# The first expert product of a two-layer decoder in a fixed order: copies and activations reordered, gates four chunks later, top-k interleaved, rows and weight chunks loaded ahead into the activations' area

## The chip, the cores and the metric

The kernel runs on one core of one Trainium2 chip. The metric is device microseconds (us) of one execution, the median of several runs. In the text TensorE is PE, VectorE is DVE, ScalarE is ACT, GpSimd is POOL and SyncE is SP; SP, ACT and POOL also issue DMAs, each from a queue of its own, in order.

## What is computed

256 tokens of width 1024 go through two layers. Each layer has a mixing half (attention, convolution, spatial gating) and a PEER half: a product-key retrieval picks 16 of 16384 single-neuron experts for each of 8 heads of a token. The change lies in the PEER half, of which this is the reference, cut:

```python
q = (t @ w_pq).reshape(T, PEER_HEADS, 2, PEER_HALF)
s = jnp.einsum('thpk,hpnk->thpn', q, sub_keys)
top_s, top_i = lax.top_k(s, PEER_TOPK)                 # two times 16 of 128 keys
cand_s = top_s[:, :, 0, :, None] + top_s[:, :, 1, None, :]
best_s, best_pos = lax.top_k(cand_s.reshape(...), PEER_TOPK)
gate = jax.nn.softmax(best_s, axis=-1)
u = expert_down[experts]                               # rows of 1024
act = gelu(einsum('td,thkd->thk', t, u))
out = einsum('thk,thkd->td', gate * act, expert_up[experts])
```

Before each half the residual is normalised and scaled by vectors that come from six products of the conditioning vector with `w_ada` (48 columns of 1024 rows in each layer).

## The kernel before

The fp32 weights are streamed once, in chunks of 128x1024 values (512 KB each), through a ring of seven buffers (`raw`). `Src.seq` lists the chunks in the order of their use: `w_ada` columns ("ada"), input, output and query projections, then 128 chunks of `down` and 128 of `up` in each layer, with the `ada` columns that are due later spread among them. Half of the `down` and `up` chunks are issued on ACT's queue, the rest on SP's.

The PEER half of a layer works in three steps.

1. Query projection and top-k. Scores of both token blocks (128 tokens each, `b` = 1 and 0) go to DVE, which finds the top 16 keys (`top_keys`), sums the candidates, finds their top 16 (`top_cand`), turns positions into indices (`ranks`, `match`, `times`, `total`) and forms the softmax (`gate`). These steps lie in one list, `fill`, of which `run_fill` releases a budget after each chunk. `to_picks` then transposes the indices and gates of a block on PE and copies them out on ACT and DVE.
2. First product. For each of 128 `down` chunks PE multiplies the chunk with T tokens (`DENSE`: 168 in the first layer, 160 in the second), two chunks to a PSUM bank (`ch`, two buffers). ACT applies the gelu and writes `acts`, 128 x T values in the `arena`, the large SBUF tile in which all regions are cut. Meanwhile the gates are spread over the experts: for a group of four tokens DVE makes one-hots (`make_onehots`, L1021), ACT scales them (L1028 to L1032, and L1034 on DVE), PE multiplies them into a PSUM bank `g` (`gate_mm`, L1044), and `gate_use` multiplies the gelus already there (DVE, L1052) or lays the gate down for those to come (ACT, L1055). `act_use` (L1072) multiplies a later gelu (L1064, into `gt`) into gates that lie there.
3. The other 88 or 96 tokens (`TS`) are not in the dense product. For each of them POOL gathers 128 expert rows of 1024 values (`fetch`, L988, an indirect DMA of 512 KB) and DVE multiplies the rows with the token (`dot`, L998). This needs the picks of block 1 in another layout (`pairs`), which they reach through DRAM (`pair_in`), and the tokens repeated over the partitions, through DRAM too (`dot_in`). Second product (`combine`): PE multiplies `up` chunks with `acts` (L1083), DVE adds the gathered `up` rows (L1013), and `folds` (L1089) joins both.

What sets the order: up to the second product the tile framework's scheduler arranges the instructions of each engine by its own estimate, and only the second product and the passages between the halves are under `manual_schedule`, in the order of the code. The numbers that the code fixes are: dots from chunk `begin` + 6 to 120, `begin` = 21; gates from `start` = 28 to chunk 124; `FILL` and `FILL_DOWN`, the budgets of `run_fill`. Both layers have the same `begin` and `start`.

Of the kernel before, what the change touches and what calls it, by code (L numbers as in the profile page):

```python
# [44 lines left out]
PICKS_LAG = 3  # L45
D_FIRST = 6
D_LAST = 120
# [3 lines left out]
FILL = 1.25  # L51
FILL_DOWN = 2.1
EARLY = (112, 116, 96, 100, 64, 68)
ADA_TAIL = 0
# [15 lines left out]
def hybrid_trunk(ctx: ExitStack, tc: tile.TileContext, x_in, c_in, vec_in, w_ada, w_in, w_out, w_pq,  # L70
# [41 lines left out]
    dot_in = [dram.tile([S - t, D], F32, name=f"dot_in{n}") for n, t in enumerate(DENSE)]  # L112
    pair_in = [dram.tile([S - t, 2, P], F32, name=f"pair_in{n}") for n, t in enumerate(DENSE)]
# [63 lines left out]
    class Src:  # L177
# [4 lines left out]
        later = []  # L182

    def dma_ahead(upto):
        while Src.loaded < min(upto, len(Src.seq)):
            kind, src, raw = Src.seq[Src.loaded]
            if kind != "early":
                raw = stream.tile([P, D], F32, name="raw", tag="raw", bufs=RAW)
# [7 lines left out]
    fill = deque()  # L196

    def run_fill(budget):
        Src.credit = min(budget, Src.credit + budget)
        while fill and Src.credit > 0:  # L200
            cost, fn = fill.popleft()
            fn()
            Src.credit -= cost
# [14 lines left out]

    def cast_step(late=None):
# [4 lines left out]
        while Src.later and Src.later[0][0] <= k + RAW - QUEUE_LAG:  # L224
            nc.scalar.dma_start(*Src.later.pop(0)[1:])
# [3 lines left out]
        if kind == "ada":  # L229
# [24 lines left out]
        dma_ahead(k + RAW)  # L254
        return True

# [28 lines left out]
    for layer in range(DEPTH):  # L285
# [3 lines left out]
        if layer == 0:  # L289
# [7 lines left out]
            body = first[:2] + body[:n] + first[2:] + mix(body[n:] + tail[:ADA_TAIL], ada(0, [2, 3, 4])) + tail[ADA_TAIL:]  # L297
# [5 lines left out]
        if layer + 1 < DEPTH:  # L303
            dn = mix(dn, ada(0, [5]) + ada(1, [0, 1]), 4, 112)
            un = mix(un, ada(1, [2, 3, 4]), 4, 120)
        else:
            dn = mix(dn, ada(1, [5]), 40, 112)
        seq += dn + un
    Src.seq = seq
    dma_ahead(RAW)  # L310
# [168 lines left out]
    def tables(layer, after=None):  # L479
# [3 lines left out]
        nc.gpsimd.dma_start(R_BIAS, rel_bias)  # L483
        nc.gpsimd.dma_start(R_SW, sgu_w[layer])
        nc.gpsimd.dma_start(R_SB, sgu_b[layer])
# [14 lines left out]
    def mixing(layer, qg, update=None, late=None):  # L500
# [245 lines left out]
        if layer == 0:  # L746
# [3 lines left out]
            qg = tables(0, R_HF[:, 4, 0:1])  # L750
# [39 lines left out]
    def retrieval(layer, update, late):  # L790
        known.clear()
        T = DENSE[layer]
        def top_keys(b, hp):
            s = R_S[:, b, hp, :]
            v = R_TS[:, b, hp * 16:(hp + 1) * 16]
            ix = R_TI[:, b, hp * 16:(hp + 1) * 16].bitcast(U32)
            scr = R_SCR[:, hp % 2, :P]
            nc.vector.max(out=v[:, :8], in_=s)
            nc.vector.max_index(out=ix[:, :8], in_max=v[:, :8], in_values=s)
            nc.vector.match_replace(out=scr, in_to_replace=v[:, :8], in_values=s, imm_value=NEG_FILL)  # L800
            nc.vector.max(out=v[:, 8:], in_=scr)
            nc.vector.max_index(out=ix[:, 8:], in_max=v[:, 8:], in_values=scr)
# [11 lines left out]

        def cand(b):
# [9 lines left out]
        def top_cand(h):  # L825
            s = R_CAND[:, h, :]
            v = best[:, h * 16:(h + 1) * 16]
            ix = pos[:, h * 16:(h + 1) * 16].bitcast(U32)
            scr = R_SCR[:, h % 2, :80]
            nc.vector.max(out=v[:, :8], in_=s)  # L830
            nc.vector.max_index(out=ix[:, :8], in_max=v[:, :8], in_values=s)
            nc.vector.match_replace(out=scr, in_to_replace=v[:, :8], in_values=s, imm_value=NEG_FILL)
            nc.vector.max(out=v[:, 8:], in_=scr)
            nc.vector.max_index(out=ix[:, 8:], in_max=v[:, 8:], in_values=scr)
# [21 lines left out]
        def times(b, j):  # L856
            nc.vector.tensor_tensor(R_OH, R_OH, R_TE[:, b, :, j], op=OP.mult)
# [14 lines left out]

        def to_picks(b):
# [4 lines left out]
            if b == 1:  # L878
# [54 lines left out]
        def rest():  # L933
# [4 lines left out]
            for b in (1, 0):  # L938
                fill.append((0.7, lambda b=b: cand(b)))
                for h in range(8):  # L940
                    fill.append((0.8, lambda h=h: top_cand(h)))
# [352 lines left out]
```

## Time and profile before

| what | value |
|---|---|
| three runs | 1674.01, 1683.61, 1679.82 us; median 1679.82 |
| the profiled execution | 1675.43 us, its span 1673.7 us |
| PE, DVE, ACT, POOL busy | 93%, 61%, 26%, 29% of the span |
| DMA | 571.24 MB, mean 341 GB/s |
| first product, layer 0 and 1 | 189.1 to 558.0 us; 1032.5 to 1386.4 us |
| second product, layer 0 and 1 | 558.0 to 879.4 us; 1386.2 to 1669.4 us |

Busy shares are over the whole span. An engine with a low share can still be the one that is waited for, since engines work through their queues in order. Each `f32` matmul shows as two instructions in the trace, so a chunk is 16 of them.

### The profile page before, as it was taken

Reading aid. Unit: us, or ns where it says so; the run is one execution under the profiler, and the core shown is the slowest. Engines: PE = TensorE matmul, PEld = TensorE weight load, DVE = VectorE, ACT = ScalarE, POOL = GpSimd, SP = SyncE. Lnnn points to the kernel's source line nnn. Section 1 sums busy time; section 2 is a strip of 40 time slices with the busy share of each in tenths; the row PEclk is TensorE's granted clock in tenths of the full one; section 3 lists DMA queues with packets and bytes.
Section 4 is the critical chain, followed back from the end, with each engine's and each line's share of the span. In section 5 each row is a group of like instructions: output and inputs, shape, how many; then the busy total and the mean of one; then the engine's idle time right before and its main releaser. Section 6 shows DMA issues by size and latency. Waiting matters only on the chain.

```text
span 1673.7 us, 28977 instructions
## 1 busy us (share of the span) xinstructions
PE 1558.0 (93%) x11240; PEld 1520.5 (91%) x11240; DVE 1017.7 (61%) x2347; ACT 438.7 (26%) x1203; POOL 490.1 (29%) x441
## 2 busy tenths in 40 slices
PE   7999997988989999898999999969988899999998
PEld 6879987888989999898999899968988899999998
DVE  6757976767874154445436679767778743444443
ACT  2346223534343000000015763134344320000000
POOL 1000214434430243433300002054454404444440
PEclk9999998999999999999999999979999999999999
DMA  9975589999998999999975454889999989999997
GB/s 387 328 258 178 163 270 353 407 411 405 406 418 273 337 418 419 396 419 408 414 282 164 135 174 148 248 314 419 416 408 419 415 289 375 419 419 419 418 419 284
DMA packets 158461, 571.24 MB, mean 341 GB/s; under 512 B 20102, under 2 KB 20502, under 8 KB 157171
## 3 DMA queue, kind: packets, MB, share of 16 engines
q1 hardware_dynamic: 63072, 229.14, 37.0%
q0 software_dynamic: 58032, 205.16, 30.8%
q10 hardware_dynamic: 37219, 135.08, 21.2%
q8 instruction: 88, 1.44, 0.3%
q14 instruction: 50, 0.41, 0.1%
HBM read 565.20 MB, written 4.09 MB: 340 GB/s over the span
## 4 chain that ended last, share of the span: by engine, by line
PE 39%; DMA 32%; issue 13%; DVE 7%; POOL 6%; ACT 2%; SPq 0%; POOLq 0%; ACTq 0%; DVEq 0%
PE ch L316 13%; DMA arena<-in_up,arena 12%; PE acc L1083 12%; DMA arena<-in_down_rows,arena 5%; POOL arena L988 4%; DMA raw<-in_w_ada 4%; DMA raw<-in_up 3%; DMA spots<-in_up,arena 3%; DMA raw<-in_down 2%; PE ch L318 2%; PE ch L319 1%; PE ch L320 1%; POOL spots L988 1%; DMA pair_in<-chosen 1%; DMA spots<-in_down_rows,arena 1%
## 5 line engine op out<-in xcount | busy, mean ns | idle before, releaser
L316 PE MATMUL ch<-arena,raw 128*128 128x160 f32 (+2 forms) x4256 | 642.9, 312 | 21.1 <-ACT arena L1061 16.5
L316 PEld LDWEIGHTS ch<-arena,raw 128*128 128x128 f32 x4256 | 619.3, 195 | 28.7 <-ACT arena L1061 18.2
L1083 PE MATMUL acc<-arena,raw 128*128 128x168 f32 (+1 forms) x4096 | 578.9, 305 | 15.0 <-DMA raw<-in_up 14.8
L1083 PEld LDWEIGHTS acc<-arena,raw 128*128 128x128 f32 x4096 | 576.1, 192 | 17.1 <-DMA raw<-in_up 16.9
L988 POOL DMA_INDIRECT arena<-in_up,arena x154 | 193.5, 1257 | 351.3 <-DVE spots L1013 108.2
L1013 DVE SCALAR_TENSOR_TENSOR spots<-arena,spots 128x1024 f32<-128x1024 f32 x150 | 192.6, 1284 | 129.5 <-DMA arena<-in_up,arena 127.5
L206 DVE SCALAR_TENSOR_TENSOR raw<-raw,arena 128x1024 f32<-128x1024 f32 x96 | 116.6, 1219 | 177.3 <-DMA raw<-in_w_ada 135.5
L988 POOL DMA_INDIRECT arena<-in_down_rows,arena x134 | 152.1, 1135 | 194.4 <-DVE arena L998 170.3
L998 DVE SCALAR_TENSOR_TENSOR arena<-arena,spots 128x1024 f32<-128x1024 f32 x134 | 163.2, 1224 | 52.9 <-DMA arena<-in_down_rows,arena 52.5
L1044 PE MATMUL g<-arena 128*128 128x128 f16 x656 | 54.0, 226 | 58.2 <-ACT arena L1055 47.1
L1061 ACT ACTIVATE arena<-ch 128x336 f32<-128x336 f32 (+35 forms) x122 | 40.7, 336 | 250.4 <-PE ch L316 190.6
L1044 PEld LDWEIGHTS <-arena 128*128 128x128 f16 x656 | 45.8, 99 | 65.5 <-issue 51.2
L318 PE MATMUL ch<-hh,hi 128*128 128x256 f32 x288 | 82.6, 289 | 2.0 <-DVE arena L436 1.9
L1028 ACT ACTIVATE arena<-arena,parts 128x128 f16<-128x128 f16 x164 | 64.5, 393 | 75.9 <-DVE arena L1021 75.9
L347 ACT ACT_TABLE_LOAD x6 | 7.7, 1283 | 292.0 <-DMA raw<-in_up 291.9
L319 PE MATMUL ch<-hh,lo 128*128 128x256 f32 x288 | 81.8, 284 | 0.0
L320 PE MATMUL ch<-hh,hi 128*128 128x256 f32 x288 | 81.7, 284 | 0.0
L988 POOL DMA_INDIRECT spots<-in_down_rows,arena x50 | 59.9, 1197 | 73.4 <-DVE spots L998 59.8
L998 DVE SCALAR_TENSOR_TENSOR spots<-spots 128x1024 f32<-128x1024 f32 x50 | 61.2, 1224 | 20.3 <-DMA spots<-in_down_rows,arena 20.2
L1021 DVE TENSOR_TENSOR arena<-iota,picks 128x1024 f16<-128x1024 f16 x82 | 56.5, 691 | 23.6 <-PE g L1044 21.8
L239 DVE TENSOR_TENSOR lo<-raw,hi 128x1024 fp32r<-128x1024 f32 x42 | 51.4, 1230 | 27.9 <-ACT hi L246 27.8
L1052 DVE SCALAR_TENSOR_TENSOR arena<-arena,g 128x112 f32<-128x112 f32 (+31 forms) x82 | 37.9, 463 | 47.6 <-ACT arena L1061 40.1
(234 smaller groups left out, 1614.1 us busy)
## 6 DMA issues: line engine op xcount, KB each, us to landing
raw<-in_down SPq DMA_DIRECT2D x128, 512.0 KB, 7.1
raw<-in_down ACTq DMA_DIRECT2D x128, 512.0 KB, 7.3
raw<-in_up SPq DMA_DIRECT2D x128, 512.0 KB, 8.0
raw<-in_up ACTq DMA_DIRECT2D x128, 512.0 KB, 8.2
raw<-in_w_ada SPq DMA_DIRECT2D x96, 512.0 KB, 7.9
raw<-in_w_pq SPq DMA_DIRECT2D x32, 512.0 KB, 3.6
raw<-in_w_in SPq DMA_DIRECT2D x26, 512.0 KB, 4.7
raw<-in_w_out SPq DMA_DIRECT2D x16, 512.0 KB, 4.6
```

Source lines behind the costliest of these rows:

```text
L206: nc.vector.scalar_tensor_tensor(raw, raw, 1.0, cact, op0=OP.mult, op1=OP.mult, accum_out=mods[layer][:, col:col + 1])
L316: nc.tensor.matmul(dst, hi[:, cols], k[0], start=start, stop=stop, **kw)
L318: nc.tensor.matmul(dst, hi[:, cols], k[0], start=start, stop=False, **kw)
L319: nc.tensor.matmul(dst, lo[:, cols], k[0], start=False, stop=False, **kw)
L320: nc.tensor.matmul(dst, hi[:, cols], k[1], start=False, stop=stop, **kw)
L988: nc.gpsimd.indirect_dma_start(out=held[n], out_offset=None, in_=rows if n >= TS else down_rows[:, :], in_offset=bass.IndirectOffsetOnAxis ...
L998: nc.vector.scalar_tensor_tensor(row, row, 1.0, R_DX[which(k)[0]], op0=OP.mult, op1=OP.mult, accum_out=R_DOTS[:, k:k + 1])
L1013: nc.vector.scalar_tensor_tensor(R_SUM[s], row, w, R_SUM[s], op0=OP.mult, op1=OP.add)
L1021: nc.vector.tensor_tensor(both, iota2[:, None, :, :].to_broadcast([P, 4, P, 2]), vals[:, :, None, :].to_broadcast([P, 4, P, 2]), op=OP.is_ ...
L1028: nc.scalar.activation(og[0][:, 0, i, :], oh[:, 0, i, :], AF.Copy, scale=parts[:, 0, t + i:t + i + 1])
L1044: nc.tensor.matmul(dst, og[j][:, i // 2, i % 2, :], on[:, i // 2, :, i % 2], start=j == 0, stop=j == 1)
L1083: nc.tensor.matmul(acc[d // 2][:, (d % 2) * S:(d % 2) * S + T], u[:, d * P:(d + 1) * P], acts[:, i, :], start=i == 0 and d % 2 == 0, stop= ...
```

## The change

The first product, too, stands under `manual_schedule`: its instructions run in the order of the code. The loop over the 128 chunks is written anew, and this goes with it:

- ACT: the gelu of a pair of chunks stands ahead of the scaling copies, which come a chunk after their one-hots (`make_onehots` is split into `compare` and `factors`). `act_use` follows a pair later, with two temporary buffers. In `gate_use` ACT's part stands ahead of DVE's. The last scaling moves from DVE to ACT (eight ACT copies in a group instead of six, and no DVE one).
- Gates start at `start` + 4, one group to a pair of chunks. `start` is 33 and 35, `begin` 11 and 12 (layer 0 and 1).
- Top-k: two key sets or four candidate sets are worked on side by side, step by step, and block 1's whole list goes ahead of block 0's.
- The DRAM detours `dot_in` and `pair_in` are replaced by copies from SBUF to SBUF on POOL's queue, one for each stretch of partitions: 2 and 2 for the first set of tokens, then 8 and 8, 16 and 16 in layer 0 (4 and 4 in layer 1).
- Rows: seven regions of the later `acts` area hold rows until the gates start, and a few regions more hold them afterwards. Dots run at 0.2 to a chunk until `start`, then 0.8 or 0.92. 83 of 88 and 94 of 96 are done in the first product, and the rest at the head of the second.
- Chunks: ten `down` chunks (numbers 4 to 13) have places of their own in the `acts` area.
- `ada`: eight columns of layer 0 move from its first product to its output projection. Layer 1's columns ("aside") use the `hi`/`lo` buffers rather than the ring: 22 in the first product of layer 0, 18 in its second, 8 in layer 1's first.

```diff
-PICKS_LAG = 3
-D_FIRST = 6
-D_LAST = 120
+PICKS_LAG = 2
+WHERE_LAG = 4
+SETS_LAG = (0, 6, 11)
+SETS_KNOWN = 17
+D_FIRST = 8
+DOT_SLOW = 0.2
+DOT_RATE = (0.8, 0.92)
+AHEAD_AT = (8, 12, 16, 36, 40, 44, 48, 52, 56, 60)
+PASSING = (36, 40, 44, 48, 52, 56, 60)
-FILL = 1.25
-FILL_DOWN = 2.1
+FILL = 1.5
+FILL_DOWN = (2.2, 2.1)
...
+            body += mix(tail[:6], ada(0, [5])) + tail[6:]
...
+        for n, at in enumerate(AHEAD_AT):
+            dn[AHEAD_FIRST + n] = ("early", dn[AHEAD_FIRST + n][1], region(at * S, D))
...
+        def spread_picks(s):
+            off, n = SETS[s]
+            for h in range(P // n):
+                nc.gpsimd.dma_start(pairs[h * n:(h + 1) * n, :, off:off + n],
+                                    chosen[T - P + off:T - P + off + n, :, h * n:(h + 1) * n])
...
+        manual.enter_context(tc.manual_schedule())
...
             chunk_mm(ps[:, j * S:(j + 1) * S], next_chunk(), T, R_HX)
-            if pend is not None:
-                act_use(*pend)
-                pend = None
             while waiting:
                 g, gp = waiting.pop(0)
                 gate_use(g, gp, 2 * pair)
                 gdone = g + 1
+            if j == 1:
+                tdone = 4 * gdone
+                pend.append((pair, gelu(pair, ps, tdone), tdone))
+                if len(pend) > 1:
+                    act_use(*pend.popleft())
+            while compared:
+                factors(compared.pop(0))
+            if make and made < NG:
+                compare(made)
+                compared.append(made)
+                made += 1
...
+                if i == begin + WHERE_LAG:
+                    where(0)
+                    known_to[0] = SETS[0][1]
+                    fetch()
...
+                if i >= begin + D_FIRST:
+                    due += DOT_SLOW if start is None else DOT_RATE[layer]
+                while dotted < min(TS, int(due), len(held)):
+                    dot(dotted)
+                    dotted += 1
...
-        manual.enter_context(tc.manual_schedule())
         late = []
-        update, qg = combine(layer, late)
+        update, qg = combine(layer, late, dotted)
```

Three places show how the order on an engine moves. The first is DVE in the middle of layer 0's first product, about two groups of gates before the change: the row dots are L998, the one-hots L1021, the gates' use L1052, the later gelus' use L1072, the scaling L1034.

```order
L998 SCALAR_TENSOR_TENSOR spots,arena<-spots 128x1024
L1021 TENSOR_TENSOR arena<-iota_85,picks 128x1024
L1052 SCALAR_TENSOR_TENSOR arena<-arena,g 128x62x4
L1072 TENSOR_TENSOR arena<-arena,gt 128x2x60
L1034 TENSOR_TENSOR arena<-arena,parts 128x256
L998 SCALAR_TENSOR_TENSOR arena<-arena,spots 128x1024 x3
L1052 SCALAR_TENSOR_TENSOR arena<-arena,g 128x64x4
L1021 TENSOR_TENSOR arena<-iota_85,picks 128x1024
L1072 TENSOR_TENSOR arena<-arena,gt 128x2x64
```

The same place on DVE after the change; L1048 is the dot, L218 an `ada` column, L1107 the gates' use, L1125 the later gelus' use and L1071 the one-hots.

```order
L1048 SCALAR_TENSOR_TENSOR spots,arena<-spots 128x1024
L218 SCALAR_TENSOR_TENSOR aside,mod_108<-aside,arena 128x1024
L1107 SCALAR_TENSOR_TENSOR arena<-arena,g 128x60x4
L1125 TENSOR_TENSOR arena<-arena 128x2x44
L1071 TENSOR_TENSOR arena<-iota_85,picks 128x1024
L1048 SCALAR_TENSOR_TENSOR arena<-arena,spots 128x1024 x2
L1107 SCALAR_TENSOR_TENSOR arena<-arena,g 128x62x4
L1125 TENSOR_TENSOR arena<-arena 128x2x48
```

Each pair now has the same order, gates, gelus, one-hots, dots, with one or two dots between two uses of gates where up to three stood; the scaling is gone from DVE, and the dots come last in their pair.

The second place is PE at the first gates of layer 0, before the change: the transposes of block 1's and block 0's picks (L876), `down` chunks (L316, here eight rows of `x` to a chunk), and the first gate products (L1044).

```order
L316 MATMUL ch<-arena,raw 128x168 x120
L876 MATMUL g<-ident,arena 128x128 x3
L316 MATMUL ch<-arena,raw 128x168 x64
L876 MATMUL g<-ident,arena 128x128 x3
L316 MATMUL ch<-arena,raw 128x168 x16
L1044 LDWEIGHTS arena
```

The same place on PE after the change (L918 the transposes, L345 the chunks, L1097 the gate products); chunks that lie in the arena alone are those loaded ahead.

```order
L345 MATMUL ch<-arena,raw 128x168 x8
L345 MATMUL ch<-arena 128x168 x80
L918 MATMUL g<-ident,arena 128x128 x3
L345 MATMUL ch<-arena,raw 128x168 x152
L918 MATMUL g<-ident,arena 128x128 x3
L345 MATMUL ch<-arena,raw 128x168 x48
L1097 LDWEIGHTS arena
```

Between the last picks and the first gates stood two chunks, and six stand there now; block 1's picks come nineteen chunks ahead of block 0's instead of eight.

The third place is SP's queue from the output projection of layer 0 to its first product, before the change.

```order
L192 DMA raw<-in_w_ada 128x1024 x3
L192 DMA raw<-in_w_out 128x1024 x8
L192 DMA raw<-in_w_pq 128x1024 x16
L192 DMA raw<-in_down 128x1024 x4
L192 DMA raw<-in_w_ada 128x1024
```

A piece of the same stretch after the change, in which the chunks loaded ahead are those that go to the arena.

```order
L204 DMA raw<-in_w_ada 128x1024 x2
L204 DMA raw<-in_w_out 128x1024 x2
L204 DMA raw<-in_w_pq 128x1024 x9
L204 DMA arena<-in_down 128x1024 x2
L204 DMA raw<-in_w_pq 128x1024 x2
L204 DMA arena<-in_down 128x1024 x2
```

The ten chunks now stand among the loads of the input, output and query projections (three, two and five of them), with projection weights behind them in the same queue.

More of the change, by code (lines that the diff above doesn't have):

```diff
@@ L962, in experts, with release @@
         R_DROW = spots[:, 3, :]
-        free = deque([spots[:, n, :] for n in range(len(SETS), 4)] + [region(108 * S, D)])
+        beyond = [region(at * S, D) for at in (80, 84) if at * S >= P * T]
+        passing = [region(at * S, D) for at in PASSING]
+        free = deque([spots[:, n, :] for n in range(len(SETS), 3)] + [region(108 * S, D)] + beyond + passing)
         held = {}
+        known_to = [0]
+        retired = []
+        def release(row):
+            if not any(row is r for r in retired):
+                free.append(row)
         def dot_rows():
@@ L1062, in gelu @@
             if tdone:
[L1063 removed]
+                tmp = region(120 * S + pair % 2 * 2 * T, 2, T)
                 nc.scalar.activation(tmp[:, :, :tdone], v[:, :, :tdone], AF.Gelu)
@@ L1152, in experts @@
                 start = i + 1
-                make_onehots(0)
-                make_onehots(1)
+                for g in range(2):
+                    compare(g)
+                    compared.append(g)
                 made = 2
                 sent = 0
-            elif start is not None:
-                want = min(NG, -(-NG * (i + 1 - start) // (G_LAST - start)))
+                free.extend(SLOTS_OPEN)
+            elif start is not None and i >= start + 4:
+                want = min(NG, -(-NG * (i - 3 - start) // (G_LAST - 4 - start)))
@@ L1173, in experts @@
-            if begin == i:
-                where()
-                fetch()
-            if start == i + 1:
-                free.extend(SLOTS_OPEN)
-                fetch()
-            if begin is not None:
-                while dotted < min(TS, -(-TS * (i - begin - D_FIRST + 1) // (D_LAST - begin - D_FIRST))):
+                    make = True
+            if not retired and begin is not None and len(fills[0]) <= RETIRE:
+                retired.extend(passing)
+                for row in [row for row in free if any(row is r for r in passing)]:
+                    free.remove(row)
@@ L1183, in experts @@
                     if dotted == TS:
-                        dot_acts()
-            if j == 1:
-                tdone = 4 * gdone
-                pend = (pair, gelu(pair, ps, tdone), tdone)
-        if pend is not None:
-            act_use(*pend)
+                        dot_acts(0, TS)
+            if start is not None and i % 4 == 3:
+                run_aside()
+        while pend:
+            act_use(*pend.popleft())
         while waiting:
```

254 lines of the change are left out of this document (152 added, 102 removed).

## Prediction

> **What bounds the kernel now.** I read the windows by stage first, for busy time, granted clock and what the DMAs moved (the count in brackets is of instructions).
>
> ```profile
> 98.00:132.00 34.00, 31.61 (x232) 29.99 (x232) 17.03 (x28) 14.14 (x23) 0.56 (x1) 0.95 0.59 194
> 152.00:189.10 37.10, 37.10 (x316) 37.10 (x315) 35.46 (x179) 16.06 (x23) 6.39 (x9) 1.00 0.49 154
> 189.10:276.80 87.70, 74.72 (x504) 73.73 (x502) 65.04 (x305) 16.29 (x33) 24.39 (x28) 0.94 0.85 278
> 276.80:505.00 228.20, 204.03 (x1520) 200.91 (x1521) 173.84 (x350) 101.41 (x342) 91.47 (x81) 0.95 1.01 406
> 505.00:558.00 53.00, 51.79 (x386) 51.36 (x385) 17.70 (x34) 13.54 (x50) 1.59 (x2) 1.00 0.77 250
> 558.00:879.40 321.40, 306.43 (x2099) 304.25 (x2098) 140.58 (x146) 7.29 (x14) 100.56 (x89) 0.97 0.98 393
> 1032.50:1105.00 72.50, 55.20 (x405) 54.28 (x404) 49.33 (x275) 13.62 (x26) 15.98 (x21) 0.91 0.73 216
> 1105.00:1345.00 240.00, 216.38 (x1667) 213.03 (x1668) 179.04 (x359) 101.92 (x346) 111.07 (x95) 0.96 1.02 414
> 1345.00:1386.30 41.30, 41.23 (x321) 41.12 (x321) 19.14 (x32) 10.44 (x39) 1.64 (x2) 1.00 0.83 263
> 1386.30:1669.40 283.10, 282.08 (x2081) 281.70 (x2080) 118.23 (x98) 0.44 (x1) 123.16 (x91) 1.00 0.98 399
> 1450.00:1550.00 100.00, 100.00 (x738) 100.00 (x738) 43.64 (x34) 0.00 (x0) 47.72 (x35) 1.00 1.03 419
> ```
>
> The last row shows that PE and the DMAs can both be full at once: 100.00 us busy at 419 GB/s. In the first products they take turns: while the top-k runs PE stalls and the DMAs are at 278 and 216 GB/s; then the DMAs are full (406, 414) and PE stalls; at the end PE is full and the DMAs idle again (250, 263).
>
> What PE needs, from its timeline (start, duration, instructions; 16 make a chunk):
>
> ```profile
> 244.27 18.41 PE L316 MATMUL ch<-arena,raw 128*128 128x168 f32 x128
> 569.73 46.56 PE L1083 MATMUL acc<-arena,raw 128*128 128x168 f32 x325
> 1080.51 8.86 PE L316 MATMUL ch<-arena,raw 128*128 128x160 f32 x64
> 1361.25 8.91 PE L316 MATMUL ch<-arena,raw 128*128 128x160 f32 x64
> 1370.00 0.62 PE L1044 MATMUL g<-arena 128*128 128x128 f16 x8
> 1370.46 2.39 PE L316 MATMUL ch<-arena,raw 128*128 128x160 f32 x16
> ```
>
> A chunk takes 2.30 us in layer 0. In layer 1 it takes 2.21 with the end that the pipeline adds, so I take 2.18. A gate group adds 0.46 (1370.00 to 1370.46). With 1.5 us for small products, layer 0's first product needs 128 x 2.30 + 42 x 0.46 + 1.5 = 315 us and layer 1's 128 x 2.18 + 40 x 0.46 + 1.5 = 299. They take 369 (87.7 + 228.2 + 53) and 354: 54 and 55 us above PE's need. Layer 0's second product needs about 128 x 46.56 / 325 x 16 = 293 and some 6 for the folds, and takes 321; layer 1's second product has no stall.
>
> Where the 54 and 55 us go:
>
> ```profile
> 225.73 7.82 PE L316 MATMUL ch<-arena,raw 128*128 128x168 f32 x32 [2.81 <-DMA raw<-in_down]
> 239.31 4.80 PE L316 MATMUL ch<-arena,raw 128*128 128x168 f32 x32 [0.64 <-DMA raw<-in_down]
> 262.84 4.73 PE L316 MATMUL ch<-arena,raw 128*128 128x168 f32 x32
> 280.72 5.95 PE L316 MATMUL ch<-arena,raw 128*128 128x168 f32 x32
> 1066.12 4.58 PE L316 MATMUL ch<-arena,raw 128*128 128x160 f32 x32 [0.44 <-DMA raw<-in_down]
> 1071.41 5.81 PE L316 MATMUL ch<-arena,raw 128*128 128x160 f32 x41 [0.72 <-DMA raw<-in_down]
> 1105.06 6.58 PE L316 MATMUL ch<-arena,raw 128*128 128x160 f32 x32 [15.69 <-ACT arena L1061]
> ```
>
> *Early waits for chunks*: from 225.73 to 239.31 run four chunks, 13.6 us instead of 9.2, and 2.8 us of idle stand ahead: 7 in layer 0. Layer 1 has two short ones (0.44, 0.72) with slow starts around them, some 3 by what is left over. *The end of the top-k*: after 262.84 + 4.73 PE waits until 276.8 (then two gate groups run), 13 us with a slow start; in layer 1 15.7 and a slow chunk pair (6.58 for 4.4), 18. *The rest*, 34 in either layer, is the row-fed stretch.
>
> Who is waited for there (total, times, longest), with the dots' own duration and the price of POOL's small DMAs:
>
> ```profile
> DVE arena L981 <- DMA pairs<-pair_in: 24.4, 2, 17.9
> ACT picks L889 <- DVE picks L888: 31.8, 3, 20.2
> PE g L1044 <- ACT arena L1055: 47.1, 25, 5.6
> ACT arena L1055 <- DVE arena L1052: 59.8, 57, 4.2
> DVE arena L998 <- DMA arena<-in_down_rows,arena: 52.5, 42, 3.3
> DVE spots L998 <- DMA spots<-in_down_rows,arena: 20.2, 18, 4.5
> L998 DVE SCALAR_TENSOR_TENSOR arena<-arena,spots 128x1024 f32<-128x1024 f32 x66 | 80.4, 1225 | 25.3 <-DMA arena<-in_down_rows,arena 25.2
> 243.98 3.85 POOL L886 DMA_DIRECT2D pairs<-pair_in  x6 [4.51 <-DMA pair_in<-chosen]
> ```
>
> Read upwards: a dot waits for its row, the gates' use behind it on DVE waits, ACT's part waits for DVE's, and PE for the PSUM bank. At the top-k's end, DVE sits 17.9 us in front of `pairs` coming through DRAM, with block 1's picks behind it; ACT waits for those 20.2 us, with the gelus behind it, and PE for the gelus.
>
> **The change, part by part.** *Demand of the row-fed stretch.* The issues of chunks in the page give the size of one:
>
> ```profile
> raw<-in_down SPq DMA_DIRECT2D x128, 512.0 KB, 7.1
> ```
>
> At 419 GB/s that is 1.251 us, and rows and columns are as large. Before, 88 rows in 93 chunks and 24 `ada` columns in 108 make 1 + 0.95 + 0.22 = 2.17 transfers to a chunk, 2.71 us, against PE's 2.30 + 42/96 x 0.46 = 2.50. Layer 1: 1 + 1.03 + 0.11 = 2.14, 2.68 us, against 2.37. After: 1 + 0.8 + 0.2 (a column to five chunks) = 2.50 us against 2.30 + 0.23 = 2.53, and 1 + 0.92 = 2.40 against 2.41. DMA and PE are level, as in the last window, so most of the 34 goes. I leave 10 in each layer, since DVE still waits in order: bounds 0 (that window) and 34. Gain 24 + 24.
>
> DVE's own load, from its groups in the first product of layer 0:
>
> ```profile
> L1021 DVE TENSOR_TENSOR arena<-iota,picks 128x1024 f16<-128x1024 f16 x40 | 27.6, 689 | 10.0 <-PE g L1044 8.6 <-ACT gt L1064 1.0 <-issue 0.2
> L1052 DVE SCALAR_TENSOR_TENSOR arena<-arena,g 128x112 f32<-128x112 f32 (+41 forms) x42 | 19.4, 463 | 24.7 <-ACT arena L1061 20.9 <-ACT gt L1064 2.2 <-PE g L1044 1.5
> L1072 DVE TENSOR_TENSOR arena<-arena,gt 128x32 f32<-128x32 f32 (+41 forms) x49 | 16.4, 335 | 17.6 <-ACT gt L1064 17.6
> ```
>
> In a pair of chunks these make 0.69 + 0.46 + 0.34 = 1.5 us, and 1.6 dots and half a column at 1.23 another 2.6: 4.1 of 5.06 us, where nothing but order can make it late. ACT takes two more copies a group and stays off the path (101.41 of 228.20 us before).
>
> *End of the top-k.* `where` comes four chunks (9 us) after one direct copy instead of behind two hops; picks have two chunks, first gates six. This goes, bounds 0 and all of it: 13 and 18. I leave 3 in each, since DVE is nearly full in the top-k (a budget of 2.2 to a chunk of 2.30) and a pick can be late. Gain 10 + 15. The two sets' interleaving itself I cost at nothing: the same operations, and DVE has no gaps there before.
>
> *Chunks ahead.* Ten of them use the DMAs' slack before 189 us (154 GB/s). Gain 7 in layer 0 and 3 in layer 1, bounds 0 and 10. They and eight more columns stand in SP's queue among projection weights, where a region that is not free holds up the ring, and DVE does eight more columns, 10 us, in a stretch of 34 in which it is half busy (17.03). Bounds 0 and 12 (one such column for each wait); I take a loss of 5.
>
> *Copies on POOL.* 52 in layer 0 at 3.85 / 6 = 0.64 us, 33 us, with row fetches behind them. Dots go at 0.2 then, so I take 0; bounds 0 and 10, if the second `where`, which stands within block 0's top-k on DVE, has to wait.
>
> *Second products.* Five and two dots move there. In layer 0 6 columns fewer (18 for 24) offset them: 0, bounds -15 and +15, as the DMAs enter it full instead of idle at 250 GB/s. Layer 1: +2.
>
> Sum: 24 + 24 + 10 + 15 + 10 - 5 - 2 = 76 less. The profiled execution took 1675.4 us, 1673.7 of them its span (1.7 lie around it), and the median of the runs is 1679.8. From the profiled one: 1599 us.
>
> **A rule against it.** The windows from 1105 us and 1386 us show 414 and 399 GB/s over 240 and 283 us. The Trainium skill ("DMA: Bandwidth & Descriptors", section "Where 436 GB/s comes from") says that for transfers from HBM to SBUF HBM's side binds, near 358 GB/s a core. By that a transfer is 1.46 us, two of them 2.93 to a chunk of 2.53, and over 90 chunks 36 us in each layer would come back: some 1671. The trace disagrees with 419 GB/s for 100 us, so I give it no chance of its own.
>
> **Rivals.**
> - *Better, 1565.* The stretch has no remainder (-20), and layer 0's second product loses half of its 22 us (-11) and half of the top-k's remainder goes (-3): the level demand of the last window speaks for it, the unchanged rates of rows and columns in that second product against.
> - *The demand only moves, 1640.* The DMAs enter the second products a ring behind: 7 x 1.25 = 9 us in each, three more stalls of 8 us in layer 0's. For it: 393 GB/s there already. Against: layer 1's second product runs at 399 with no stall.
> - *The picks are no earlier, 1630 to 1671.* DVE falls behind in the top-k, PE waits in order at the transposes, and the 31 us stay (1630); with the row stretch's gain lost too, no change. For it: 35.46 of 37.10 us busy on DVE ahead of the first product. Against: six chunks of slack.
> - *Slower, 1690.* In fixed order every late row stops DVE with the gates, gelus and one-hots behind it. Before, 72.7 us of waits fell on 184 dots, 0.4 each; the scheduler could put other work ahead of a dot, and the code's order cannot. There are 82 pairs: from 76 / 82 = 0.9 us a pair beyond what I left, the gain is gone; at 1.1 (a wait of 3.3 us, the longest of its row, on each third pair) it is 82 x 1.1 = 90 above the forecast, 1689. Against: a row is fetched six or eight slots ahead, where five or six were there before.
>
> **How the numbers follow.** Forecast 1599: 0.55, its own range 1580 to 1618. Better 0.13; demand moves 0.12; picks no earlier 0.12, of which 0.04 within 0.5%; slower 0.08. The range from 1560 to 1650 takes in the first three and most of the fourth, with the bounds of the remainders (20 and 48 us) not all at one end. Half a per cent, 8 us, is about what a measurement here tells from no change. Faster 0.88, same 0.04, slower 0.08.
>
> **What would show it.** First products of about 333 and 320 us, without a stall of over 5 us at the first gates; DMA near 410 GB/s up to their ends, so no closing stretch at 250; DVE's waits for rows below 40 us in total; layer 0's second product within 15 us of 321. I am wrong if PE waits at the transposes of the picks, if SP's queue holds up the projections before 189 us, or if the second products grow by over 15.

## The result and the profile after

The changed kernel takes 1618.8 us (four runs, 1618.5 to 1619.4) where the kernel before takes 1681.7: ratio 0.9634, 95% interval 0.9601 to 0.9667. The forecast, 1599, lies 20 us below; the result is just above the forecast's own range (1580 to 1618) and within the wide one (1560 to 1650). The profiled execution went from 1675.4 to 1619.4 us, so 56 us are to be found in the traces. One execution of run 4 below, the profiled one (1653.7 us), was in a slower state and is left out, so the stages of that run are read from run 9, which has the same rates.

First the stages of the changed kernel, in the columns of the table of before: busy time of PE, PE's weight loads, DVE, ACT and POOL with their instructions, granted clock, share and rate of the DMAs.

```profile
98.00:132.00 34.00, 31.97 (x234) 29.98 (x233) 28.12 (x49) 13.00 (x19) 0.00 (x0) 1.00 0.97 363
268.00:298.40 30.40, 19.74 (x119) 19.16 (x118) 16.66 (x34) 8.57 (x25) 24.71 (x35) 0.78 0.64 183
298.40:523.00 224.60, 224.60 (x1762) 222.77 (x1760) 162.51 (x311) 127.85 (x448) 81.36 (x73) 1.00 1.03 417
523.00:849.60 326.60, 309.16 (x2099) 307.29 (x2098) 146.47 (x156) 7.67 (x16) 125.69 (x91) 0.96 0.97 393
1052.00:1066.00 14.00, 9.86 (x39) 8.69 (x38) 9.69 (x62) 0.44 (x1) 7.95 (x11) 0.63 1.03 417
1103.00:1313.60 210.60, 210.54 (x1717) 208.69 (x1716) 157.02 (x301) 119.71 (x428) 86.73 (x80) 1.00 1.02 410
1313.50:1585.00 271.50, 271.50 (x1999) 271.28 (x1998) 113.84 (x97) 0.92 (x3) 125.66 (x90) 1.00 1.03 418
1585.00:1613.60 28.60, 16.64 (x85) 16.26 (x83) 17.03 (x18) 0.00 (x0) 4.13 (x4) 0.64 0.38 151
```

In the two row-fed stretches (third and sixth row) PE is busy for 224.60 of 224.60 and 210.54 of 210.60 us, with the DMAs at 417 and 410 GB/s: the alternation of before is gone. Counted by the chunks' times over PE's need (2.30 and 2.18 us a chunk, 0.46 a gate group), 1 and 2 us are lost there now, where I had left 10 in each. The first row shows the stretch of the output projection, where DVE does the eight columns more (28.12 us busy, 17.03 before) and the DMAs are at 363 GB/s; the first product starts at 188.6 us for 189.1 before, so they cost nothing that shows. The lost time now lies in three short places: the end of layer 0's top-k (PE 19.74 of 30.40 us), fourteen us in layer 1's top-k (9.86 of 14.00) and the ends of the second products (16.64 of 28.60).

| stage | before | after | forecast |
|---|---|---|---|
| first product, layer 0 | 369 | 334.5 | 333 |
| second product, layer 0 | 321.4 | 326.6 | 321 |
| first product, layer 1 | 354 | 310.9 | 320 |
| second product, layer 1 | 283 | 300.1 | 285 |

PE's timeline at the first and third place, in time order (start, duration, what ran, idle time ahead and what ended it):

```profile
279.18 0.48 PE L918 MATMUL g<-ident,arena 128*128 128x128 f32 x1 [8.48 <-DVE arena L899]
281.84 0.45 PE L918 MATMUL g<-ident,arena 128*128 128x128 f32 x1 [2.19 <-DVE arena L908]
833.12 9.55 PE L1143 MATMUL acc<-fold,spots 128*128 128x8 f32 x44 [8.47 <-DVE qg L523]
1599.86 6.61 PE L1143 MATMUL acc<-fold,spots 128*128 128x32 f32 x30 [11.93 <-DVE spots L1063]
```

L918 are the transposes of block 0's picks, which wait for DVE; L1143 are the folds of the weighted `up` rows, which wait for DVE's last rows (L523 stands in DVE's queue right behind the rows). What DVE waits for at the first place, and what POOL does meanwhile:

```profile
264.66 0.17 DVE L1030 TENSOR_SCALAR arena<-pairs 128x16 uint32<-128x16 f32 x1 [5.36 <-DMA spots<-spots]
277.25 0.17 DVE L1030 TENSOR_SCALAR arena<-pairs 128x8 uint32<-128x8 f32 x1 [12.41 <-DMA pairs<-chosen]
256.02 0.50 POOL L1025 DMA_DIRECT2D pairs<-chosen  x1 [3.24 <-DMA arena<-in_down_rows,arena]
260.22 0.50 POOL L1025 DMA_DIRECT2D pairs<-chosen  x1 [3.70 <-DMA arena<-in_down_rows,arena]
271.73 4.34 POOL L1025 DMA_DIRECT2D pairs<-chosen  x8 [0.58 <-DMA pairs<-chosen]
```

A `where` turns the picks of a set of tokens into row numbers for the fetches; the first serves the first set, the second the two others. The second `where` (L1030) stands in the middle of block 0's top-k and waits 17.8 us there for the copies of the second and third set, which crawl along POOL's queue: six of the first eight wait for an earlier row to land. And DVE's waits for rows (total, times, longest):

```profile
DVE arena L1048 <- DMA arena<-in_down_rows,arena: 90.7, 84, 2.4
DVE spots L1048 <- DMA spots<-in_down_rows,arena: 14.9, 16, 2.5
DVE spots L1063 <- DMA arena<-in_up,arena: 263.6, 147, 3.7
```

DVE waits 106 us for `down` rows, more than the 72.7 of before and far from the 40 that I named as a sign, yet PE has no stall behind it.

### The profile page after: what moved, and what is told of

Read it like the earlier page. It is cut to its first block, busy times and chain, and to the rows that moved or that the text cites. A ratio compares the mean times of both kernels' runs of the same rounds, so it can differ in the third digit from the quotient of the medians.

```text
span 1617.7 us, 29030 instructions
## 1 busy us (share of the span) xinstructions
PE 1550.2 (96%) x11240; PEld 1514.8 (94%) x11240; DVE 1002.7 (62%) x2263; ACT 475.4 (29%) x1356; POOL 518.5 (32%) x467
## 4 chain that ended last, share of the span: by engine, by line
DMA 41%; PE 35%; issue 11%; POOL 6%; DVE 4%; ACT 2%; POOLq 0%; ACTq 0%; SPq 0%; DVEq 0%
DMA arena<-in_up,arena 28%; PE ch L345 18%; DMA spots<-in_up,arena 6%; POOL arena L1038 5%; DMA arena<-in_down_rows,arena 4%; PE ch L347 2%; PE ch L348 2%; PE ch L349 2%; DMA spots<-in_down_rows,arena 1%; DMA raw<-in_w_ada 1%; PE acc L1143 1%; POOL spots L1038 1%; DVE spots L1063 1%; PE ch L434 1%; PE g L936 1%
## 5 line engine op out<-in xcount | busy, mean ns | idle before, releaser
L345 PE MATMUL ch<-arena,raw 128*128 128x168 f32 (+2 forms) x3936 | 590.1, 309 | 8.2 <-issue 6.3
L345 PEld LDWEIGHTS ch<-arena,raw 128*128 128x128 f32 x3936 | 563.9, 192 | 15.5 <-issue 9.6
L1038 POOL DMA_INDIRECT arena<-in_up,arena x159 | 220.7, 1388 | 276.6 <-DMA arena<-in_up,arena 222.5
L1048 DVE SCALAR_TENSOR_TENSOR arena<-arena,spots 128x1024 f32<-128x1024 f32 x148 | 179.8, 1222 | 92.4 <-DMA arena<-in_down_rows,arena 90.7
L1081 ACT ACTIVATE arena<-arena,parts 128x128 f16<-128x128 f16 x164 | 64.6, 394 | 121.5 <-DVE arena L1071 81.2
L1114 ACT ACTIVATE arena<-ch 128x320 f32<-128x320 f32 (+30 forms) x122 | 42.0, 344 | 167.6 <-PE ch L345 141.7
L1038 POOL DMA_INDIRECT spots<-in_down_rows,arena x36 | 43.9, 1218 | 67.0 <-DVE spots L1048 47.9
L345 PE MATMUL ch<-arena 128*128 128x160 f32 (+2 forms) x384 | 62.7, 323 | 1.7 <-ACT arena L398 1.5
L218 DVE SCALAR_TENSOR_TENSOR raw<-raw,arena 128x1024 f32<-128x1024 f32 x48 | 57.8, 1215 | 9.1 <-DMA raw<-in_w_ada 5.5
L1087 ACT ACTIVATE arena<-arena,parts 128x128 f16<-128x128 f16 x164 | 63.4, 387 | 0.0
L1083 ACT ACTIVATE arena<-arena,parts 128x128 f16<-128x128 f16 x164 | 63.4, 387 | 0.0
L1085 ACT ACTIVATE arena<-arena,parts 128x128 f16<-128x128 f16 x164 | 63.4, 387 | 0.0
L345 PEld LDWEIGHTS ch<-arena 128*128 128x128 f32 x384 | 57.8, 194 | 6.0 <-ACT arena L398 4.0
```

The costliest lines, as they stand in the source:

```text
L345: nc.tensor.matmul(dst, hi[:, cols], k[0], start=start, stop=stop, **kw)
L1038: nc.gpsimd.indirect_dma_start(out=held[n], out_offset=None, in_=rows if n >= TS else down_rows[:, :], in_offset=bass.IndirectOffsetOnAxis ...
L1048: nc.vector.scalar_tensor_tensor(row, row, 1.0, R_DX[which(k)[0]], op0=OP.mult, op1=OP.mult, accum_out=R_DOTS[:, k:k + 1])
L1081: nc.scalar.activation(og[0][:, 0, i, :], oh[:, 0, i, :], AF.Copy, scale=parts[:, 0, t + i:t + i + 1])
L1083: nc.scalar.activation(og[1][:, 0, i, :], oh[:, 0, i, :], AF.Copy, scale=parts[:, 1, t + i:t + i + 1])
L1085: nc.scalar.activation(og[0][:, 1, i, :], oh[:, 1, i, :], AF.Copy, scale=parts[:, 0, t + 2 + i:t + 3 + i])
```

## The experiments

Every kernel is the changed one but for the edit shown, unless it says otherwise. The kernel before had medians of 1681.0 to 1682.3 us beside them, so medians are compared directly; the ratio to it, with its interval, stands beside each.

**1. The second `where` later.**

```diff
-SETS_KNOWN = 17
+SETS_KNOWN = 24
```

> The second `where` moves seven chunks later (24 after the first picks are known, for 17), behind the last picks. Theory A, the second `where` stops DVE in the middle of block 0's top-k (it waits 5.36 and 12.41 us for POOL's copies), and that is layer 0's stall at the first gates: the first product of layer 0 falls from 334.5 to about 323 us, layer 1's (no such stall) stays at 311, in all about 1607 us. Rival B, DVE is simply full there and the picks come when its own work allows: within 3 us of 1619. Rival C, the DMAs bound the first product, and a shorter stall only raises their debt: layer 0's first product is shorter, its second longer by as much, 1617 to 1620.

1607.2 us (1606.4 to 1607.4), ratio 0.9564 [0.9492, 0.9636]. Theory A holds in the total: 11.6 us less. In the profile PE no longer stops at the picks, but a new stall stands ten chunks later, so layer 0's first product falls only to 329.5, and the second by 6.7:

```profile
299.74 0.58 PE L1097 MATMUL g<-arena 128*128 128x128 f16 x2 [4.72 <-ACT arena L1081]
299.28 0.40 ACT L1081 ACTIVATE arena<-arena,parts 128x128 f16<-128x128 f16 x1 [11.07 <-DVE arena L1071]
293.96 1.23 DVE L1048 SCALAR_TENSOR_TENSOR arena<-arena,spots 128x1024 f32<-128x1024 f32 x1 [10.93 <-DMA arena<-in_down_rows,arena]
284.69 1.00 POOL L1038 DMA_INDIRECT arena<-in_down_rows,arena  x1 [1.09 <-DMA spots<-spots]
```

Read from below: POOL's first row fetch of the stretch stands behind the last of the 48 copies; DVE waits 10.93 us for a row, ACT 11.07 for the one-hots behind it, PE for ACT. It is the mechanism of the rival "slower", once.

**2. The first rows dripped.**

```diff
                     where(0)
-                    known_to[0] = SETS[0][1]
+                    known_to[0] = 3
                     fetch()
+                elif begin + WHERE_LAG < i < begin + SETS_KNOWN:
+                    known_to[0] = min(SETS[0][1], known_to[0] + 1)
+                    fetch()
```

> Rows of the first set are fetched three at first and then one to a chunk, instead of nine to eleven at once. Theory A, that burst takes the DMAs from the other queues and gives the slow chunks (three in layer 1, 13 us for 4.5; some 4 us in layer 0): layer 1's first product falls from 310.9 to about 302, layer 0's from 334.5 to 331, in all about 1607 us. Rival B, the slow chunks belong to the place in the program and not to the burst: they stay, within 3 us of 1619. Rival C, what the burst fetched early is missed at the end of the top-k, and the row-fed stretch starts behind: 1622 to 1630.

1613.8 us (1611.9 to 1615.0), ratio 0.9601 [0.9529, 0.9674]. Layer 1's first product falls to 302.7, as theory A says; layer 0's does not (335.6): its slow chunks go too, but chunk 32, with the wait for the picks in it, takes 19.1 us for 13.9, and the gain is gone. DVE in its timeline:

```profile
278.44 0.17 DVE L1030 TENSOR_SCALAR arena<-pairs 128x8 uint32<-128x8 f32 x1 [20.84 <-DMA pairs<-chosen]
```

So in layer 0 the time of the picks is set by POOL's copies; a PE that is earlier only waits longer.

**3. Folds behind the last chunk.**

```diff
-HELD = 2
+HELD = 0
...
-                if i == 125:
-                    for d in range(DC):
-                        folds(d)
             for d in range(DC):
-                for i, u in last:
-                    add(i, d, u)
+                folds(d)
```

> The folds stand behind all 128 chunks of the second product, instead of between chunk 125 and the last two. Theory A, the rows of `up` come late because the DMAs enter the second product in debt; the last two chunks' products then cover part of DVE's lag: PE's wait at the folds (8.5 us in layer 0, 11.9 in layer 1) falls to 2 and 5, in all about 1606 us. Rival B, the rows wait for the last chunks' own transfers, which come no earlier, and what follows the folds (the updates) was covered by the two held chunks: the wait is the same or moves to the updates, 1615 to 1622.

1605.1 us (1604.2 to 1606.3), ratio 0.9552 [0.9480, 0.9624]: 13.7 less, theory A. The waits at the folds:

```profile
832.11 8.29 PE L1143 MATMUL acc<-fold,spots 128*128 128x8 f32 x40 [3.99 <-DVE qg L523]
1593.59 6.61 PE L1143 MATMUL acc<-fold,spots 128*128 128x32 f32 x30 [6.92 <-DVE spots L1063]
```

They halve (8.47 and 11.93 before the edit), since PE does the last two chunks meanwhile. From the start of layer 0's second product to that of layer 1's first it is 475.0 us for 479.8, from that of layer 1's second to the end 296.9 for 304.2. DVE's lag itself is still there.

**4. Faster dots, the demand of before.**

```diff
-DOT_RATE = (0.8, 0.92)
+DOT_RATE = (0.95, 1.05)
```

> Dots of the row-fed stretch go at 0.95 and 1.05 to a chunk, instead of 0.8 and 0.92, so that none is left to the second products and the demand on the DMAs is about that of before. Theory A, the gain came from levelling the demand: 1 + 0.95 + 0.2 = 2.15 transfers make 2.69 us to a chunk against PE's 2.53 for some 75 chunks, 12 us longer in layer 0's first product, about 11 in layer 1's, and some 10 of it back in the second products: about 1632 us. Rival B, the gain came from the looser order (copies behind the gelus, products a pair later), and the demand did not matter: first products within 4 us of 334.5 and 310.9, the second products shorter by 7 rows, about 1611 us.

1629.8 us (median of four executions, 1628.3 to 1637.3), ratio 0.9715 [0.9636, 0.9793]: 11.0 more, theory A.

**5. The product with gelu(ch) at its old place.**

```diff
+            while pend:
+                act_use(*pend.popleft())
             while waiting:
                 ...
             if j == 1:
                 tdone = 4 * gdone
                 pend.append((pair, gelu(pair, ps, tdone), tdone))
-                if len(pend) > 1:
-                    act_use(*pend.popleft())
```

> The product with gelu(ch) goes back to the first place behind the pair's second chunk, ahead of the gates' copy and product, instead of a pair later and behind them; all else as in the changed kernel. Theory A, the levelled demand on the DMAs is what keeps PE busy in the row-fed stretch, and the order has slack: first products within 4 us of 334.5 and 310.9, in all 1615 to 1624 us. Rival B, the loose ties are what lets DVE wait for rows without PE: DVE stands for ACT's gelu (about 0.5 us) and PE's last chunk in each of some 82 pairs with the gates' use behind it, 0.3 to 0.5 us a pair, 25 to 40 us in all: 1640 to 1660 us.

1619.2 us (1617.2 to 1622.3), ratio 0.9629 [0.9605, 0.9654]: no difference, theory A. "Products a pair later" earns nothing here. The profile has another lesson: layer 1's slow chunks at 1052 us are gone, though in layer 1 nothing ahead of them was edited, and yet its first product takes 311.5, for the picks are late instead:

```profile
1082.00 0.27 PE L918 MATMUL g<-ident,arena 128*128 128x128 f32 x1
1087.89 0.48 PE L918 MATMUL g<-ident,arena 128*128 128x128 f32 x1 [5.61 <-DVE arena L899]
1085.88 0.18 DVE L1030 TENSOR_SCALAR arena<-pairs 128x32 uint32<-128x32 f32 x1 [14.79 <-DMA pairs<-chosen]
1066.71 0.58 POOL L1025 DMA_DIRECT2D pairs<-chosen  x1 [4.13 <-DMA arena<-in_down_rows,arena]
```

The burst of rows costs layer 1 its 9 us either way: as slow chunks, or as copies that wait for eleven rows to land.

**6. No chunks ahead.**

```diff
-AHEAD_AT = (8, 12, 16, 36, 40, 44, 48, 52, 56, 60)
+AHEAD_AT = ()
```

> No chunks ahead in the acts area: those ten chunks go through the ring again, in each layer. Theory A (the prediction's term), only the early waits come back, 7 us in layer 0 and 3 in layer 1: about 1629 us. Rival B, the ten transfers are taken out of a stretch in which the DMAs have slack and come back in one where they are full, 10 x 1.25 = 12.5 us in each layer, up to 25 in all: 1640 to 1645 us. Rival C, the stall at the end of the top-k covers the loss in layer 0 and the debt is repaid at the folds: within 4 us of 1619.

1623.0 us (1620.6 to 1624.4), ratio 0.9651 [0.9629, 0.9673]: 4.2 more, at the edge of rival C. The first product starts 2.7 us later (191.3), and no early wait comes back: before chunk 32, the one with the wait for the picks, no chunk takes over 3.3 us. A difference of 4 us is about the runs' own spread (1617.2 to 1622.3 in run 5). As in run 5, the slow chunks of both layers are gone and the picks are late in their place: chunk 32 of layer 0 takes 20.3 us for 13.9, chunk 34 of layer 1 9.3.

**7. The edits of 1, 2 and 3 together.**

> The later second `where`, the dripped first rows and the folds behind the last chunk together. Theory A, the three stalls are separate and their gains add: -11.6 -5 -13.7 = 1588.5 us, or 1585 if layer 0's part of the drip (4 us, which the wait at the second `where` took up before) now shows. Rival B, they share one slack (the DMAs, at 410 to 420 GB/s from 298 to 523 us), and each further gain is smaller: 1593 to 1600 us. The stall of 9 us at chunk 42 of layer 0 that came with the later `where` stays by both: its rows are still issued behind POOL's 48 copies.

1595.8 us (1594.8 to 1596.5), ratio 0.9484 [0.9464, 0.9504]: rival B's range. They are not separate: the drip lets PE reach chunk 42 earlier and chunk 42, with the wait in it, takes 19.7 us for 9.3. Layer 0's first product takes 334.9 us, no less than in the changed kernel; the gain is layer 1's and the folds'.

**8. Copies one to a chunk, and their `where` 60 chunks after the first picks** (with the drip and the folds last). `spread_picks` and `dot_spread` get an argument for one copy.

```diff
-SETS_KNOWN = 17
+SETS_KNOWN = 60
...
+        copies = deque((fn, s, part) for s in range(1, len(SETS)) for fn in (spread_picks, dot_spread)
+                       for part in range(P // SETS[s][1]))
...
                 free.extend(SLOTS_OPEN)
+                fetch()
...
-                for s in range(1, len(SETS)):
-                    if i == begin + SETS_LAG[s]:
-                        spread_picks(s)
-                        dot_spread(s)
+                if i >= begin + SETS_LAG[1] and copies:
+                    fn, s, part = copies.popleft()
+                    fn(s, part)
```

> As the one before, but the copies of the second and third set go one to a chunk, from six chunks after the first picks, and their `where` stands 60 chunks after them. Theory A, layer 0's 9 us stall at chunk 42 comes from POOL's copies ahead of the row fetches: layer 0's first product falls from about 329 to 320 us, in all about 1577 us. Rival B, a copy in each chunk, with its wait for an earlier row's landing (1.4 to 3.7 us each), delays the row fetches of the stretch: layer 0's first product no shorter, DVE's waits for rows in it longer, 1585 to 1600 us.

1589.6 us (1585.5 to 1591.8), ratio 0.9454 [0.9432, 0.9476]. Layer 0's first product falls to 320.4 as theory A says, and up to 300 us PE is in it without a gap. PE's timeline at block 0's picks, and the windows from its start:

```profile
265.98 0.49 PE L918 MATMUL g<-ident,arena 128*128 128x128 f32 x3
266.30 13.85 PE L345 MATMUL ch<-arena,raw 128*128 128x168 f32 x96
```

```profile
188.60:300.00 111.40, 111.40 (x806) 111.20 (x806) 88.18 (x370) 33.27 (x87) 43.98 (x54) 1.00 0.77 277
300.00:509.00 209.00, 207.55 (x1605) 204.72 (x1604) 150.88 (x291) 116.84 (x412) 87.45 (x90) 0.99 1.03 412
508.90:814.70 305.80, 297.29 (x2052) 295.46 (x2051) 141.02 (x147) 3.56 (x6) 124.24 (x91) 0.99 1.02 417
```

The total is in B's range all the same, though the profiled execution, of span 1583.8 us, is the fastest of the four: A is right on the stall and wrong on the sum. Layer 0's first product is over 14 us shorter than in run 7, and the profiled spans differ by 11.0, for from there to layer 1's first product it is 471.7 us for 467.5. It beats both kernels: 29 us under the changed one.

**9. Faster dots and the early product together.** The edits of 4 and 5.

> The faster dots (0.95 and 1.05 to a chunk) and the early product with gelu(ch) together, to see whether the order matters once the rows are late. Apart they gave 1631 and 1619 us. Theory A, they are independent: 1628 to 1634 us. Rival B, a late row in front of the product on DVE now holds the next pair's PSUM bank: 10 to 25 us more, 1640 to 1656 us, and that would be the part of before's 34 us a layer that the demand alone does not give.

1627.8 us (1622.9 to 1631.6), ratio 0.9664 [0.9629, 0.9699]: theory A, they are independent. Its stages show what the faster dots do:

```profile
300.00:539.80 239.80, 233.63 (x1752) 223.07 (x1751) 172.28 (x328) 124.47 (x449) 97.22 (x80) 1.00 1.02 414
1120.00:1338.90 218.90, 210.99 (x1648) 203.03 (x1648) 154.22 (x295) 118.24 (x426) 91.85 (x83) 0.99 1.02 409
1338.80:1600.00 261.20, 259.22 (x1888) 258.18 (x1888) 119.02 (x94) 0.44 (x1) 118.68 (x88) 0.99 1.02 415
```

The DMAs stay at 414 and 409 GB/s, and PE now waits. The first products are 15.5 and 15.6 us longer (350.0, 326.5) than in the changed kernel, the second ones 7.0 and 13.2 shorter (319.6, 286.9).

**10. The first product left to the scheduler.**

```diff
-        manual.enter_context(tc.manual_schedule())
         begin = None
 ...
+        manual.enter_context(tc.manual_schedule())
         late = []
```

> The changed kernel's code, with the first product left to the scheduler, which orders each engine's instructions by its own estimates, as before the change; chunks, dots' rates, columns and picks stay. Theory A, the levelled demand does it and any order with as much slack is as good: 1614 to 1626 us. Rival B, the fixed order earns what the faster dots did not take back (34 - 13 us in layer 0, 34 - 16 in layer 1): about 1655 us, with PE's stalls spread over the row-fed stretch as before.

1642.5 us (1640.7 to 1644.8), ratio 0.9765 [0.9735, 0.9796]: 23.6 more, between the theories and nearer to B. The first products take 344.0 and 349.0, the second ones 314.1 and 286.2. Windows of the row-fed stretches, and who waits for whom:

```profile
300.00:532.60 232.60, 220.87 (x1697) 217.66 (x1696) 145.36 (x283) 124.83 (x437) 93.98 (x79) 0.99 0.97 376
1120.00:1348.70 228.70, 212.20 (x1671) 209.55 (x1670) 131.11 (x252) 115.72 (x407) 80.19 (x68) 0.98 0.93 357
```

```profile
PE g L1097 <- DVE arena L1107: 26.5, 12, 4.4
DVE arena L1107 <- ACT arena L1114: 68.1, 37, 4.2
```

At the same rates of rows and columns the DMAs are at 376 and 357 GB/s only, and PE waits for the gates' use on DVE (L1107), which waits for ACT's gelu (L1114). In the fixed order these two rows are absent from the waits: there the longest waits of PE for DVE are at the picks and the folds. Of the 48 us by which the first products are longer, layer 1 has 38; in layer 0 the row-fed stretch loses 18 too, but the wait of chunk 32 is not there.

**11. Version 8 without the chunks ahead.** The edit of 6.

> The version with late sets, dripped rows and folds last (1589.6 us), without the chunks ahead. In the changed kernel they were worth 4 us. Theory A, there the wait at the end of layer 0's top-k took up the rest; with that wait gone they are worth the prediction's 10 us: about 1600 us. Rival B, they are worth 4 us here too, mostly the first chunk of layer 0: 1592 to 1595 us.

1587.7 us (1585.5 to 1590.8), ratio 0.9441 [0.9411, 0.9472]: no loss at all; both theories miss. Layer 0's first product ends 3.4 us later than in 8 (512.4), the next layer's starts at the same time (981.0 for 980.6).

**12. Version 8 with layer 0's last columns spread further.**

```diff
-        un = mix(un, aside[len(ASIDES_AT[layer]):], 4, 100)
+        un = mix(un, aside[len(ASIDES_AT[layer]):], 4, 118)
```

> The same version, with the 18 columns of layer 0's second product spread to chunk 118 instead of 100. Theory A, PE's waits for chunks 95 to 101 there (8 us) come from a demand above 419 GB/s up to chunk 100; 18 x 18/118 = 2.7 transfers of 1.25 us fewer by then, 3.4 us: about 1586 us. Rival B, they come from the 2.4 MB of tables and of x that stand in SP's queue at chunks 89 to 102, and columns only move: 1588 to 1592 us.

1588.5 us (1586.5 to 1589.6), ratio 0.9439 [0.9409, 0.9469]: no difference, which is B's range. The second product of layer 0 does get shorter, 300.9 for 305.8 us, a little more than A says, but what it saves turns up as a wait at the folds, 2.28 us in version 8 and 7.37 here (PE's timelines, first of 8, then of this one):

```profile
817.31 7.30 PE L1143 MATMUL acc<-fold,spots 128*128 128x8 f32 x44 [2.28 <-DVE spots L1063]
```

```profile
818.94 9.55 PE L1143 MATMUL acc<-fold,spots 128*128 128x8 f32 x44 [7.37 <-DVE qg L523]
```

## Why the prediction was right, and where its terms were off

| term | forecast gain | measured | read from |
|---|---|---|---|
| row-fed stretches | 24 + 24 | 32 + 32 | chunks' times: 33 and 34 us over PE's need before, 1 and 2 after |
| end of the top-k, layer 0 | 10 | -1 | 14 us lost at chunks 32 and 33, 13 before |
| end of the top-k, layer 1 | 15 | 18, less 9 for slow chunks | chunks 22 and 23 |
| early waits, chunks ahead | 7 + 3 | about 3 + 2 | chunks' times; layer 0's after 4 of loss in its own slow chunks (21, 22, 25) |
| SP's queue, projections | -5 | 0 | 188.6 for 189.1 |
| copies on POOL | 0 | 11.6 of loss, counted in layer 0's top-k | run 1 |
| second products | 0, -2 | -5, -17 | stages |

The measured gains add up to 55 of the 56 us. That the total is only 20 us off is partly luck: 16 us more than forecast in the row-fed stretches pay for most of what the second products lost.

*The row-fed stretches* were right in kind and too small: of the remainder of 10 in each layer 1 and 2 are there, and of the projections' 5 nothing. The reason given, a level demand, is one part of it. Taking the level away (run 9) costs 31 us in the first products, taking the fixed order away at the level demand (run 10) 48; in the whole time it is 9 and 24. No run takes both away, so how they share the gain is open. The prediction weighed the fixed order as a danger only ("the scheduler could put other work ahead of a dot"); here the scheduler's order is the slower one. The rate of 410 to 418 GB/s held over 200 us and more in three windows of the changed kernel. The Trainium skill ("DMA: Bandwidth & Descriptors", section "Where 436 GB/s comes from") puts HBM's side near 358 GB/s a core; no window here shows that limit.

*The end of layer 0's top-k* is the step that failed, through "copies on POOL", taken at 0 with a bound of 10 should the second `where` have to wait. It waited 17.8 us in the middle of the picks' chain, and run 1 puts the price at 11.6. I had counted 52 copies at 0.64 us and not what each waits for in its queue. "Without a stall of over 5 us at the first gates" holds to the letter, but the sign "wrong if PE waits at the transposes of the picks" came true in layer 0, 8.48 us.

*The end of layer 1's top-k* gained 18, its whole wait, and slow chunks that no term foresaw took 9 back; run 2 removes them. No run takes the direct copies, the interleaving or the order of the two lists back, so which of them earned the 18 is not shown.

*The second products* are the other: 20 us over the sum. The second one of layer 1 grew by 17, over the 15 that I named as a limit. Both layers enter it with the DMAs full and the rows late, and PE pays at the folds (8.47 and 11.93 us), as the rival "the demand only moves" has it, though not by three stalls of 8 in layer 0: PE's waits for `up` chunks there fell from 14.8 to 9.0 us. Runs 9 and 10 show the exchange from the other side: first products longer by 31 and 48 us give second ones shorter by 20 and 26.

*Parts that earn nothing here:* products a pair later (run 5), and the chunks ahead once layer 0's picks are on time (run 11). The prediction put the gain at the early waits down to the chunks ahead, and that is not what the runs show: without them the waits stay away too (run 6). What keeps the early waits away without them is not settled; eight columns fewer stand in layer 0's stretch too.

*The signs:* 334.5 and 310.9 us for 333 and 320; DMAs at 410 GB/s and more to the ends, no closing stretch at 250; DVE's waits 106 us and not under 40, which cost PE nothing in the row-fed stretches; layer 0's second product 5 us from 321. The rival "better" had the first half of its case, almost no remainder; the versions of runs 8, 11 and 12 lie 9 to 11 us below 1599. A slip in the rivals: "the picks are no earlier" adds the full 31 us to a forecast that had left 6 of them there already, so its lower end is 1624 and not 1630.

## What to carry to other kernels

Where DMAs and PE are both near full, set the rate of the optional transfers so that each unit of PE's work has its share, and write the order by hand with a chunk or two between producer and consumer: here each cost time when it was taken away, and waits of 106 us on a side engine then held PE up nowhere in the row-fed stretches. An index, a copy or a `where` for work that is due much later does not belong in the middle of a chain that PE will wait for, and a small copy can wait in its queue for large transfers ahead of it, here up to 4.1 us each time. Time won in a stretch that the DMAs fill came back in part in the next as late data, so look at the end of the next stage and place there what can wait least last.

## What the hardware showed

*Gaps on PE and DVE beside a burst of row fetches.* In layer 1's top-k of the changed kernel, with eleven row fetches issued in a row, PE and DVE ran one or two instructions at a time, with gaps most of which no semaphore explains ("issue"). PE's timeline there; then eight microseconds of it as a window, of the changed kernel; then the corresponding eight with the rows dripped (run 2):

```profile
1055.76 0.69 PE L345 MATMUL ch<-arena,raw 128*128 128x160 f32 x2 [1.02 <-issue]
1057.20 0.69 PE L345 MATMUL ch<-arena,raw 128*128 128x160 f32 x2 [0.75 <-issue]
1059.32 8.90 PE L345 MATMUL ch<-arena,raw 128*128 128x160 f32 x40 [1.42 <-issue]
```

```profile
1052.00:1060.00 8.00, 3.91 (x16) 2.75 (x14) 3.93 (x30) 0.00 (x0) 5.87 (x7) 0.71 1.03 419
```

```profile
1053.00:1061.00 8.00, 8.00 (x61) 8.00 (x60) 7.93 (x60) 1.15 (x3) 2.91 (x6) 1.00 1.03 414
```

PE and DVE are busy for half of the time in the first window and all of it in the second, at nearly the same DMA rate. What differs is the queue that moves the bytes, POOL's with 80.4% of the DMA engines' time against 56.5% (packets, MB and share of the queue from 1052 to 1060 us, of the changed kernel and of run 2):

```profile
q0 software_dynamic: 722, 2.63, 80.4%
```

```profile
q0 software_dynamic: 526, 1.80, 56.5%
```

The share may be an effect as well as a cause, since chunks that PE does not use up free no buffer for the next. In runs 5 and 6 the same burst left no such gaps. The Trainium skill ("Runtime: NRT & Kernel Launch", section "Instruction fetch mechanics") says that each engine's sequencer fetches its instructions over a DMA queue of its own and that this is mostly hidden; the trace does not show that it was not hidden here. In the changed kernel the queues of kind "instruction" (q8 and q14) have no packet between one that starts at 1042.1 us and one at 1061.0, and PE and DVE run on within that time, PE in full from 1059.3. The cause of the gaps stays open.

*Small copies behind large ones.* A copy of 8 KB from `chosen` to `pairs` took POOL 0.5 us to issue and waited up to 4.1 us ahead of that (run 5), by the profile's account for a row of 512 KB to land, which touches neither tile; why it waits, no run shows. With the rows dripped and the copies one to a chunk (run 8), PE no longer waits for them.
